# The FFN of a decoder block: four groups begin with one token half, weight blocks summed by DMA, outputs written by parts

## The chip, the cores and the metric

One Trainium2 chip, one of its cores. The metric is the device time of one execution in microseconds (us). Lower is better. Engine names as in the profile: PE is TensorE, DVE VectorE, ACT ScalarE, POOL GpSimd, SP SyncE. PE's clock has two levels, 2.4 and 1.2 GHz; the profile gives the granted share of the upper one.

## The reference, cut to what matters

The block is attention (two branches, gated, with a residual) followed by a SwiGLU FFN. B=1, 512 tokens, width 2048, FFN width 5632, all float32. Only the last part is touched:

```python
merged = sigmoid(gl_a) * (y_a @ w_proj_mla) + sigmoid(gl_b) * (y_b @ w_proj_sb)
x = x + gt1 * (merged @ w_out)
h2 = _rms(x, g_norm2) * (1 + sc2) + sh2
gate, up = jnp.split(h2 @ w_ffn_in, 2, axis=-1)
x = x + gt2 * ((silu(gate) * up) @ w_ffn_out)
```

## The kernel before

Both products of the FFN are done by one level of Strassen's scheme in Winograd's form: with the input split in blocks X11, X12 (first 256 tokens, lower and upper half of the channels), X21, X22 (second 256 tokens) and the weights in W11, W12, W21, W22, seven products of sums of blocks take the place of eight. The seven are named P1, P5, P7, P3, P6, P2, P4 in the order in which they run. P1 is X11 W11 and P2 is X12 W21, so P1 + P2 is one finished block, C11: the gate of the first token half. The other five need sums of blocks of both token halves (X[1] to X[4]) and four sums of weight blocks.

`ffn_in_group(g)` runs over 11 groups g of FFN columns (stage "a"); `ffn_out_chunk(ci, q)` over five chunks of groups, CH=((0,1,2),(3,4),(5,6),(7,8),(9,10)), times two halves q of the output columns (stage "b"). A **piece** is one 128x1024 weight tile of a product: 4 per product and group in stage a, one per product and group in stage b; 308 and 154 in all. For each piece SP loads a raw tile (512 KB, 10 buffers `rp2`), ACT casts it (`whi`), DVE computes the rest (`wlo` = raw - whi), and PE does 12 matmuls of 512 columns (`mm3`: three per product of a float32 pair of high and low parts). `ahead_to(i, 2, 6)` sets the order: tiles are made two pieces ahead and loaded six ahead; whi and wlo have three buffers each. For P5, P7, P6 and P4 `piece_make` first subtracts one raw tile from another on DVE, so each weight block is loaded once for its group and stays until its last use.

Between the pieces stand functions put in by `add_do`: bank copies, the gate times up, and `act_back1`/`act_back2`, which transpose a group's result, make its block sums and park them in DRAM (`apark`, stores by POOL); stage b fetches them (`yb`, by SP). `at_product(n, fn)` puts a function ahead of product n. With it the norms are placed: `norm2(k, th)` scales and shifts channel tile k of token half th, `x_sums(k)` makes X[1] to X[4] from two such tiles. `first_norms` does tiles 0 to 7 of the first half; `second_norms`, at product 3 (a piece counts as a product there), does everything else at once: 24 norms and 8 sets of sums. The transposes and final sums `out_tiles(q, col_)` come after all seven products of the last chunk for a q.

Names in rows: `x12h`, `x34h` and `x12l`, `x34l` are high and low parts of X[1], X[2] and of X[3], X[4]; `x` is the part of X11 and X12; `xr` the residual; `diag` belongs to the second half's rstd; `ps_s`, `ps_t`, `ps_mm`, `ps_y` are PSUM banks; `xo` the residual at the end. L82 is the helper that records every operation.

Of the kernel before, what the change touches and what calls it, by code (L numbers as in the profile page):

```python
# [87 lines left out]
def kernel(  # L88
# [982 lines left out]
    X = {}  # L1071

# [64 lines left out]
    raws = {}  # L1137
# [15 lines left out]
    def raw_load(key):  # L1153
        if key in raws:
            return
        r = st["rp2"].tile([P, 1024], F32, tag="raw2", name=nm("raw2"))
# [42 lines left out]
    cur = {"load": 0, "make": 0}  # L1199
# [43 lines left out]
    def ffn_in_group(g, order):  # L1243
        G = {}
        n = KD // 4

# [64 lines left out]
        product("P2", "A", False, True)  # L1311
# [62 lines left out]
    ffn_in_group(0, None)  # L1374
# [5 lines left out]

    at_product(1, lambda: last_sum(1))
    at_product(2, lambda: last_row(1))

    def second_norms():
        for k in range(8):
            norm2(k + 8, 0)
            norm2(k, 1)
            norm2(k + 8, 1)
            x_sums(k)
    at_product(3, second_norms)  # L1390
    for g in range(1, FG):
        ffn_in_group(g, None)
# [20 lines left out]
    def ffn_out_chunk(ci, q):  # L1413
# [17 lines left out]
        for prod in ORDER:  # L1431
# [21 lines left out]
    def finish(q, prod, t):  # L1453
        get = lambda n: acc[q, n, t]
        if prod == "P6":
            u = get("P6")
# [4 lines left out]
            c12 = get("P3")
            vec.tensor_tensor(c12, c12, u, ALU.add)
            fin[q, 2, 2, t], fin[q, 1, 2, t] = z, c12
        if prod == "P2":
            fin[q, 1, 1, t] = get("P2")
        if prod == "P4":
            c = get("P4")
            vec.tensor_tensor(c, c, get("P6"), ALU.add)
            fin[q, 2, 1, t] = c

    def out_tiles(q, col_):
        xr_ = {}
# [120 lines left out]
```

## Time and profile before

| | |
|---|---|
| median of 3 runs | 2693.76 us (2691.06 to 2694.64) |
| the profiled execution's own time | 2691.3 us |
| its span, first to last instruction | 2689.6 us |
| busy: PE, DVE, ACT, POOL | 96%, 75%, 43%, 6% of the span |
| FFN: stage a, stage b | about 1304 to 2230, 2230 to 2690 us |
| granted PE clock, mean | 0.985 |

Busy shares are means over the span. What a change in one stage is worth is read from that stage: which engine PE waits for there, and for how long.

### The profile page before, as it was taken

The page shows a single profiled execution, that of the slowest core. Times are in us where ns is not written, and L with a number is a line of the kernel's source. Part 1 is how long each engine was busy: PE and PEld are TensorE (multiplying, and loading weights), DVE is VectorE, ACT ScalarE, POOL GpSimd, SP SyncE. Part 2 cuts the span into 40 slices and gives each one's busy share as a digit, 9 for nine tenths or more (in the row PEclk, how much of TensorE's full clock was granted, in tenths as well). Part 3 has the DMA queues.
Part 4 walks back from the last instruction along what each step waited for, and adds up shares of the span by engine and source line. Part 5 has one row for each costly group of instructions (what it writes and reads, how often), then busy time and mean ns, then how long its engine had stood idle before and what let it go on. Part 6 is the DMA issues. An engine that isn't in the chain of part 4 may idle for free.

```text
span 2689.6 us, 32101 instructions
## 1 busy us (share of the span) xinstructions
PE 2584.3 (96%) x12166; PEld 2147.2 (80%) x12166; DVE 2024.8 (75%) x2614; ACT 1149.4 (43%) x1557; POOL 154.9 (6%) x256
## 2 busy tenths in 40 slices
PE   6999999999999999999779999999999999999997
PEld 4788888888899888888558888888888887888885
DVE  8966766657877854533768888888888887689997
ACT  4434655542333322222545544455544445543331
POOL 0000000000110100000001100111110111000001
PEclk9999999999999999999879999999999999999998
DMA  9854444336666783332325445445444549765562
GB/s 341 300 195 164 160 150 143 128 134 235 252 248 251 263 347 141 141 141 98 94 63 167 144 136 160 158 144 172 151 136 151 164 135 327 235 210 193 189 206 79
DMA packets 236579, 487.29 MB, mean 181 GB/s; under 512 B 15428, under 2 KB 159044, under 8 KB 211336
## 3 DMA queue, kind: packets, MB, share of 16 engines
q1 hardware_dynamic: 215552, 426.03, 46.5%
q0 software_dynamic: 14816, 48.51, 5.0%
q10 hardware_dynamic: 6056, 10.70, 1.0%
q8 instruction: 95, 1.56, 0.2%
q14 instruction: 60, 0.49, 0.1%
HBM read 425.93 MB, written 59.24 MB: 180 GB/s over the span
## 4 chain that ended last, share of the span: by engine, by line
PE 71%; issue 17%; DVE 6%; DMA 3%; ACT 2%; POOL 0%; SPq 0%; POOLq 0%; ACTq 0%; DVEq 0%
PE ps_mm L82 48%; PE ps_s L82 11%; PE ps_t L82 8%; PE ps_y L82 5%; DMA raw<-in_w_ff_dram 2%; DVE wlo L82 2%; DVE raw L271 1%; ACT whi L82 1%; DVE s L82 0%; DVE raw L82 0%; DMA gpark<-sg 0%; DMA raw<-in_w_ada_dram 0%; POOL out_dram L1487 0%; DVE x L82 0%; DVE xr L82 0%
## 5 line engine op out<-in xcount | busy, mean ns | idle before, releaser
L82 ACT CAST whi<-raw 128x1024 fp32r<-128x1024 f32 x672 | 702.8, 1050 | 1037.7 <-PE ps_mm L82 471.6
L82 DVE TENSOR_TENSOR wlo<-raw,whi 128x1024 fp32r<-128x1024 f32 x672 | 815.7, 1218 | 341.2 <-ACT whi L82 338.5
L82 DVE TENSOR_TENSOR raw<-raw,raw 128x1024 f32<-128x1024 f32 x264 | 319.2, 1220 | 20.9 <-DMA raw<-in_w_ff_dram 17.7
L82 PE MATMUL ps_mm<-hl,whi 128*128 128x512 f32 x832 | 327.2, 393 | 0.0
L82 PE MATMUL ps_mm<-hh,whi 128*128 128x512 f32 x832 | 325.0, 391 | 0.0
L82 PE MATMUL ps_mm<-hh,wlo 128*128 128x512 f32 x832 | 324.9, 390 | 0.0
L271 DVE CUSTOM_DVE_ANT_0 raw<-raw,cb,cols 128x2048 f32<-128x2048 f32 x96 | 224.5, 2344 | 0.7 <-DMA raw<-in_w_ada_dram 0.7
L82 PE MATMUL ps_s<-whi,x 128*128 128x512 f32 x704 | 218.6, 392 | 0.1
L82 PEld LDWEIGHTS ps_mm<-hh,wlo 128*128 128x128 f32 x832 | 156.2, 188 | 32.7
L82 PEld LDWEIGHTS ps_mm<-hl,whi 128*128 128x128 f32 x832 | 156.6, 188 | 30.4
L82 PEld LDWEIGHTS ps_mm<-hh,whi 128*128 128x128 f32 x832 | 156.4, 188 | 30.5
L82 PEld LDWEIGHTS ps_s<-whi,x 128*128 128x128 f32 x704 | 133.3, 189 | 28.1 <-DVE x L82 0.6
L82 PE MATMUL ps_s<-wlo,x 128*128 128x512 f32 x352 | 139.3, 396 | 1.8 <-ACT x L82 1.8
L82 PE MATMUL ps_mm<-whi,yb 128*128 128x512 f32 x440 | 137.0, 393 | 0.0
L82 PE MATMUL ps_s<-whi,yb 128*128 128x512 f32 x352 | 108.5, 389 | 0.0
L82 PE MATMUL ps_t<-whi,yb 128*128 128x512 f32 x352 | 108.5, 389 | 0.0
L82 PE MATMUL ps_mm<-whi,x 128*128 128x512 f32 x352 | 108.4, 389 | 0.0
L82 PE MATMUL ps_t<-wlo,x12h 128*128 128x512 f32 x176 | 74.0, 421 | 30.5 <-ACT x12h L82 30.5
L82 PE MATMUL ps_mm<-mgl,whi 128*128 128x512 f32 (+1 forms) x272 | 102.7, 377 | 0.0
L82 PE MATMUL ps_mm<-mgh,whi 128*128 128x512 f32 (+1 forms) x272 | 102.4, 377 | 0.0
L82 PE MATMUL ps_mm<-mgh,wlo 128*128 128x512 f32 (+1 forms) x272 | 102.4, 377 | 0.0
L82 PEld LDWEIGHTS ps_mm<-whi,yb 128*128 128x128 f32 x440 | 83.5, 190 | 17.5
(363 smaller groups left out, 5147.6 us busy)
## 6 DMA issues: line engine op xcount, KB each, us to landing
raw<-in_w_ff_dram SPq DMA_DIRECT2D x264, 512.0 KB, 5.4
raw<-in_w_ada_dram SPq DMA_DIRECT2D x96, 1024.0 KB, 5.1
yb<-apark SPq DMA_DIRECT2D x154, 256.0 KB, 5.7
raw<-in_w_gate_dram SPq DMA_DIRECT2D x27, 1024.0 KB, 4.9
raw<-in_w_sb_dram SPq DMA_DIRECT2D x24, 1024.0 KB, 4.9
raw<-in_w_out_dram SPq DMA_DIRECT2D x16, 1024.0 KB, 4.8
raw<-in_w_gate_dram SPq DMA_DIRECT2D x24, 512.0 KB, 4.9
raw<-in_w_lat_dram SPq DMA_DIRECT2D x8, 1024.0 KB, 8.2
```

Of the source, the lines that this page charges most:

```text
L82: ins = f(*a, **kw)
L271: tc.keep_in_program_order(nc.vector.tensor_tensor_reduce(raw, raw, cb, 1.0, col(C_B + 16 * ADA[name] + j), ALU.mult, ALU.add, dst))
```

## The change

There are three edits. **Early products.** NPRE = 4: for groups 0 to 3 P1 and P2 are run ahead of everything else of the FFN (E1, E2; order E1 of group 0, E1 of 1, E2 of 0, E2 of 1, then groups 2 and 3 alike): 32 pieces, which read the first token half alone. Their results (`p1` = P1, `s1` = silu of P1 + P2) are kept for group 0 and parked in DRAM (`epark`) for groups 1 to 3: 12 stores of 256 KB by POOL, 12 loads by SP. The norms are spread: the upper channel tiles of the first half over products 3 to 6, `second_norms(k)` one k at every third product from 7 on. The groups 0 to 3 then run F5, P7, P3, P6, P4, 20 pieces each; F5 is P5 with a load of W11 of its own. **Weight sums by DMA.** The subtractions on DVE (264) are gone. A tile of W11 gets W12, then W22, then W21 added by DMAs that POOL issues with `accum_op=ALU.add`, each after the tile's casts and before the next product's (P5, P6, P4); P7's tile is a load of W12 plus an add of W22. That is 264 adds in place of the subtractions and 16 for F5, and 16 loads more. Signs of the sums of X and of the result change with it (`ngt2` = -gt2). **Outputs.** In the last chunk the final sums are cut: `out_load` fetches the residual after P5 and P6; column half 1 and token half 1 of column half 0 are written after P2, the rest after P4, in 256-column tiles. PE has as many instructions as before.

```diff
+NPRE = 4
...
+    ngt2 = cp.tile([P, KD], F32, name="ngt2")
+    def minus_gt2():
+        vec.tensor_scalar(ngt2, ada["gt2"], -1.0, None, ALU.mult)
+    step(minus_gt2)
...
         s12, s34 = t2("s12"), t2("s34")
-        vec.tensor_tensor(s12[:, lo], a[:, hi], b[:, hi], ALU.add)
-        vec.tensor_tensor(s12[:, hi], s12[:, lo], a[:, lo], ALU.subtract)
+        vec.tensor_tensor(s12[:, lo], b[:, hi], a[:, hi], ALU.subtract)
+        vec.scalar_tensor_tensor(s12[:, hi], s12[:, lo], -1.0, a[:, lo], ALU.mult, ALU.subtract)
...
+    def raw_tile(key, r=None):
         src, km = raw_src(key)
-        sync_dma(r.rearrange("p (a b) -> p a b", b=128 if km else 256), src)
-        raws[key] = r
+        new = r is None
+        if new:
+            r = st["rp2"].tile([P, 1024], F32, tag="raw2", name=nm("raw2"))
+        dst = r.rearrange("p (a b) -> p a b", b=128 if km else 256)
+        if new:
+            sync_dma(dst, src)
+        else:
+            nc.gpsimd.dma_start(dst, src, accum_op=ALU.add)
+        return r
...
     PROD = {
-        "P1": ((1, 1), "11", None), "P5": (1, "12", "11"), "P7": (3, "22", "12"), "P3": (4, "22", None),
-        "P6": (2, "22", "11"), "P2": ((1, 2), "21", None), "P4": ((2, 2), "21", "22"),
+        "P1": ((1, 1), "a", "11", True), "P5": (1, "a", "+12", True), "P7": (3, "b", "12+22", False),
+        "P3": (4, "b", "22", False), "P6": (2, "a", "+22", True), "P2": ((1, 2), "b", "21", False),
+        "P4": ((2, 2), "a", "+21", False),
+        "E1": ((1, 1), "a", "11", False), "E2": ((1, 2), "b", "21", False),
+        "F5": (1, "a", "11+12", True),
     }
-    INTO = {"P5": "11", "P7": "12", "P6": "22", "P4": "21"}
-    LAST = {"P7": ("12",), "P6": ("11",), "P4": ("21", "22")}
-    def piece_keys(stage, g, prod, j):
-        _, x, y = PROD[prod]
-        return [(stage, g, b, j) for b in (y, x) if b]
-    def piece_make(stage, g, prod, j):
-        _, x, y = PROD[prod]
-        key = (stage, g, x, j)
-        if y:
-            kd = (stage, g, INTO[prod], j)
-            vec.tensor_tensor(raws[kd], raws[key], raws[stage, g, y, j], ALU.subtract)
-            key = kd
-        r = raws[key]
+    raws = {}
...
+    def piece_load(i):
+        stage, g, prod, j = pieces[i]
+        _, tl, blk, keep = PROD[prod]
+        if blk[0] != "+":
+            raws[i] = raw_tile((stage, g, blk[:2], j))
+    def piece_add(i):
+        stage, g, prod, j = pieces[i]
+        raw_tile((stage, g, PROD[prod][2][-2:], j), raws[i])
...
+    def piece_make(i):
+        stage, g, prod, j = pieces[i]
+        _, tl, blk, keep = PROD[prod]
+        key = (stage, g, blk[-2:], j)
+        r = raws.pop(i)
         hi = wp.tile([P, 1024], F32R, tag="whi", name=nm("whi"), bufs=3)
         lo = wp.tile([P, 1024], F32R, tag="wlo", name=nm("wlo"), bufs=3)
         v4 = lambda t: t.rearrange("p (k m c) -> p k m c", k=2, m=4)
         act.copy(v4(hi), kmc(key, r))
         vec.tensor_tensor(v4(lo), kmc(key, r), v4(hi).bitcast(F32), ALU.subtract)
-        for b in LAST.get(prod, ()):
-            del raws[stage, g, b, j]
+        if keep:
+            n = next(n for n in range(i + 1, len(pieces))
+                     if pieces[n][:2] == (stage, g) and pieces[n][3] == j and PROD[pieces[n][2]][2][0] == "+")
+            raws[n] = r
+            piece_add(n)
...
     def ahead_to(i, n_make, n_load):
-        while cur["load"] < min(i + n_load + 1, len(pieces)) or cur["make"] < min(i + n_make + 1, len(pieces)):
-            if cur["load"] <= cur["make"] or cur["load"] < min(i + n_load + 1, len(pieces)):
-                for key in piece_keys(*pieces[cur["load"]]):
-                    raw_load(key)
+        end = len(pieces)
+        while cur["load"] < min(i + n_load + 1, end) or cur["make"] < min(i + n_make + 1, end):
+            if cur["load"] < min(i + n_load + 1, end):
+                piece_load(cur["load"])
                 cur["load"] += 1
             else:
-                made[cur["make"]] = piece_make(*pieces[cur["make"]])
+                while cur["add"] < min(cur["make"] + 4, cur["load"]):
+                    if "+" in PROD[pieces[cur["add"]][2]][2][1:]:
+                        piece_add(cur["add"])
+                    cur["add"] += 1
+                made[cur["make"]] = piece_make(cur["make"])
                 cur["make"] += 1
...
+    def ffn_in_early(g, i):
+        G = groups.setdefault(g, {})
+        prod = ("E1", "E2")[i]
+        for j in range(KD // 4):
+            def use(w, j=j):
+                if i == j == 0:
+                    G["A"] = tb(*(("s", "s"), ("t", "t"))[g % 2])
+                for kk in range(2):
+                    prod_mm(G["A"], X[PROD[prod][0], 2 * j + kk], w, kk, i == 0 and j == 0 and kk == 0,
+                            i == 1 and j == KD // 4 - 1 and kk == 1)
+            add_piece(("a", g, prod, j), use)
+        def out():
+            for t in range(2):
+                x = t2(("p1", "s1")[i])
+                act.activation(x, G["A"][t], (AF.Copy, AF.Silu)[i])
+                if g > 0:
+                    nc.gpsimd.dma_start(epark[g, i, t], x)
+                else:
+                    G[("p1", "s1")[i], t] = x
+        add_do(out)
...
-        product("P1", "A", True, False)
-        copy_to("p1", "A")
-        if g > 0:
+        if early and g > 0:
+            add_do(lambda: fetch_early("p1"))
+        elif not early:
+            product("P1", "A", True, False)
+            copy_to("p1", "A")
+        if g > 0 and not early:
             add_do(lambda: act_back2(g - 1))
-        product("P5", "B", True, False)
+        product("F5" if early else "P5", "B", True, False)
         copy_to("z", "B")
+        if g > 0 and early:
+            add_do(lambda: act_back2(g - 1))
...
+        if not early:
+            product("P2", "A", False, True)
+        elif g > 0:
+            add_do(lambda: fetch_early("s1"))
         both(after_p2)
...
+    for g in range(0, NPRE, 2):
+        for i in range(2):
+            ffn_in_early(g, i)
+            ffn_in_early(g + 1, i)
+    for g in range(FG):
+        ffn_in_group(g, g < NPRE)
...
+    def second_norms(k):
+        norm2(k, 1)
+        norm2(k + 8, 1)
+        x_sums(k)
...
-    def second_norms():
-        for k in range(8):
-            norm2(k + 8, 0)
-            norm2(k, 1)
-            norm2(k + 8, 1)
-            x_sums(k)
-    at_product(3, second_norms)
-    for g in range(1, FG):
-        ffn_in_group(g, None)
+    for k in range(8):
+        at_product(3 + k // 2, lambda k=k: norm2(k + 8, 0))
+        at_product(7 + 3 * k, lambda k=k: second_norms(k))
...
+            if final and prod == "P5":
+                add_do(lambda: out_load(q, 1))
+            if final and prod == "P6":
+                add_do(lambda: out_load(q, 0))
+            if final and prod == "P2":
+                add_do(lambda: out_tiles(q, 1, (0, 1)))
+                add_do(lambda: out_tiles(q, 0, (0,)))
+            if final and prod == "P4":
+                add_do(lambda: out_tiles(q, 0, (1,)))
...
+            xr = xres[m]
+            cs = slice(256 * rows[0], 256 * rows[-1] + 256)
+            vec.scalar_tensor_tensor(xr[:, cs], o[:, cs], (ngt2 if col_ == 0 else ada["gt2"])[:, m:m + 1], xr[:, cs], ALU.mult, ALU.add)
+            (nc.gpsimd if q == 0 or rows[-1] == 0 else nc.sync).dma_start(outT[m * P:(m + 1) * P, cs], xr[:, cs])
...
-                for col_ in (1, 0):
-                    add_do(lambda q=q, col_=col_: out_tiles(q, col_))
```

**DVE, the norms and the sums of X.** Before, a stretch of the norms in group 0, at the sums of the second k (`xr` scaled and shifted, `s` and `x12l`, `x34l` the sums):

```order
L82 TENSOR_TENSOR x34l_10888<-s_1890_10878,x34h_10887 128x512
L82 SCALAR_TENSOR_TENSOR xr_9996<-xr_9996,ada_gs_182,rstd_10596 128x256
L82 SCALAR_TENSOR_TENSOR x_10892<-xr_10194,ada_sh_183,x_10892 128x256
L82 SCALAR_TENSOR_TENSOR x_10899<-xr_10194,ada_sh_183,x_10899 128x256
L82 SCALAR_TENSOR_TENSOR xr_10524<-xr_10524,ada_gs_182,rstd_10596 128x256
L82 SCALAR_TENSOR_TENSOR xr_10062<-xr_10062,ada_gs_182,rstd_10596 128x256
L82 TENSOR_TENSOR s_1897_10903<-xr_9666,xr_10194 128x256
L82 SCALAR_TENSOR_TENSOR xr_10592<-xr_10592,ada_gs_182,rstd_10596 128x256
L82 TENSOR_TENSOR s_1897_10903<-s_1897_10903,xr_9666 128x256
L82 TENSOR_TENSOR wlo_11077<-raw_1845_10628,whi_11076 128x1024
L82 TENSOR_TENSOR x12l_10908<-s_1897_10903,x12h_10907 128x512
L82 TENSOR_TENSOR s_1898_10904<-xr_9666 128x256
```

After, the sums of the first k:

```order
L83 TENSOR_TENSOR wlo_10981<-raw_1884_10860,whi_10980 128x1024
L83 SCALAR_TENSOR_TENSOR x_10999<-xr_10141,ada_sh_183,x_10999 128x256
L83 TENSOR_TENSOR wlo_11020<-raw_1889_10888,whi_11019 128x1024
L83 TENSOR_TENSOR s_1912_11003<-xr_10141,xr_9614 128x256
L83 SCALAR_TENSOR_TENSOR s_1912_11003<-s_1912_11003,xr_9614 128x256
L83 TENSOR_TENSOR wlo_11044<-raw_1896_10920,whi_11043 128x1024
L83 TENSOR_TENSOR x12l_11008<-s_1912_11003,x12h_11007 128x512
L83 TENSOR_TENSOR s_1913_11004<-xr_9614 128x256
L83 SCALAR_TENSOR_TENSOR s_1913_11004<-xr_10141,s_1912_11003 128x256
L83 TENSOR_TENSOR wlo_11062<-raw_1903_10950,whi_11061 128x1024
L83 TENSOR_TENSOR x34l_11014<-s_1913_11004,x34h_11013 128x512
```

Before, 39 rows stand between the `wlo` shown and the one ahead of it; after, a `wlo` stands behind every one to three rows of the norms.

**POOL, end of group 4 and start of group 5.** Before (`apark` stores of two column tiles, nothing else):

```order
L1328 DMA apark_322<-y34h_13562 128x2x256
L1328 DMA apark_322<-y34l_13563 128x2x256
L1328 DMA apark_323<-y1h_14029 128x2x256
L1328 DMA apark_323<-y1l_14030 128x2x256
L1328 DMA apark_324<-y1h_14042 128x2x256
L1328 DMA apark_324<-y1l_14043 128x2x256
L1358 DMA apark_323<-x_2510_14135 128x512
L1328 DMA apark_323<-y12h_14143 128x2x256
```

After (`raw` are the weight tiles that get an add):

```order
L1170 DMA raw_2550_14265<-in_w_ff_dram 128x4x256
L1170 DMA raw_2555_14287<-in_w_ff_dram 128x4x256
L1170 DMA raw_2492_13984<-in_w_ff_dram 128x4x256
L1170 DMA raw_2495_14002<-in_w_ff_dram 128x4x256
L1170 DMA raw_2500_14026<-in_w_ff_dram 128x4x256
L1394 DMA apark_336<-y1h_14109 128x2x256
L1394 DMA apark_336<-y1l_14110 128x2x256
L1394 DMA apark_337<-y1h_14122 128x2x256
L1170 DMA raw_2503_14044<-in_w_ff_dram 128x4x256
L1394 DMA apark_337<-y1l_14123 128x2x256
```

The first rows are the adds of P7 of group 5, the next three and the last but one those of its P5; the stores of `act_back1` of the group before, which wait for DVE, stand among them.

**DVE, the end of the program.** Before (`acc` sums of products, `xo` the residual, read from PSUM and scaled by gt2):

```order
L82 TENSOR_TENSOR acc_18758<-acc_18758,ps_mm_20992 128x512
L82 TENSOR_TENSOR acc_18760<-acc_18760,ps_mm_20993 128x512
L82 TENSOR_TENSOR acc_18758<-acc_18758,acc_18623 128x512
L82 TENSOR_TENSOR acc_18760<-acc_18760,acc_18625 128x512
L82 SCALAR_TENSOR_TENSOR xo_21170<-ps_mm_21178,ada_gt_184,xo_21170 128x512
L82 SCALAR_TENSOR_TENSOR xo_21172<-ps_y_21185,ada_gt_184,xo_21172 128x512
L82 SCALAR_TENSOR_TENSOR xo_21174<-ps_mm_21192,ada_gt_184,xo_21174 128x512
L82 SCALAR_TENSOR_TENSOR xo_21176<-ps_y_21199,ada_gt_184,xo_21176 128x512
L82 SCALAR_TENSOR_TENSOR xo_21206<-ps_mm_21214,ada_gt_184,xo_21206 128x512
L82 SCALAR_TENSOR_TENSOR xo_21208<-ps_y_21221,ada_gt_184,xo_21208 128x512
L82 SCALAR_TENSOR_TENSOR xo_21210<-ps_mm_21228,ada_gt_184,xo_21210 128x512
L82 SCALAR_TENSOR_TENSOR xo_21212<-ps_y_21235,ada_gt_184,xo_21212 128x512
```

After:

```order
L83 SCALAR_TENSOR_TENSOR xo_21086<-ps_mm_21268,ada_gt_184,xo_21086 128x512
L83 SCALAR_TENSOR_TENSOR xo_21088<-ps_y_21275,ada_gt_184,xo_21088 128x512
L83 SCALAR_TENSOR_TENSOR xo_21212<-ps_mm_21282,ngt_315,xo_21212 128x256
L83 SCALAR_TENSOR_TENSOR xo_21214<-ps_y_21287,ngt_315,xo_21214 128x256
L83 SCALAR_TENSOR_TENSOR xo_21216<-ps_mm_21292,ngt_315,xo_21216 128x256
L83 SCALAR_TENSOR_TENSOR xo_21218<-ps_y_21297,ngt_315,xo_21218 128x256
L83 TENSOR_TENSOR acc_18839<-acc_18839,ps_mm_21096 128x512
L83 TENSOR_TENSOR acc_18841<-acc_18841,ps_mm_21097 128x512
L83 SCALAR_TENSOR_TENSOR xo_21212<-ps_mm_21328,ngt_315,xo_21212 128x256
L83 SCALAR_TENSOR_TENSOR xo_21214<-ps_y_21333,ngt_315,xo_21214 128x256
L83 SCALAR_TENSOR_TENSOR xo_21216<-ps_mm_21338,ngt_315,xo_21216 128x256
L83 SCALAR_TENSOR_TENSOR xo_21218<-ps_y_21343,ngt_315,xo_21218 128x256
```

Before, eight tiles of 512 columns follow the last sums of products; after, four halves of 256 columns do, and the other tiles stand ahead of P4's two `acc` rows.

## Rows read from the trace of the kernel before

**Rows 1.** The page: busy time by engine; TensorE's busy tenths in 40 slices.
```profile
PE 2584.3 (96%) x12166; PEld 2147.2 (80%) x12166; DVE 2024.8 (75%) x2614; ACT 1149.4 (43%) x1557; POOL 154.9 (6%) x256
...
PE   6999999999999999999779999999999999999997
```

**Rows 2.** TensorE's waits, 1150 to 2690: total us, times, longest us.
```profile
PE ps_t L82 <- ACT x12h L82: 30.5, 7, 5.9
PE ps_mm L82 <- DVE wlo L82: 19.0, 15, 5.7
...
PE ps_y L82 <- DVE xo L82: 8.6, 5, 3.8
```

**Rows 3.** TensorE's timeline, start of the FFN: start, us, instruction, [wait before].
```profile
1304.25 0.28 PE L82 MATMUL ps_mm<-mgh,wlo 128*128 128x256 f32 x1
...
1306.31 0.50 PE L82 MATMUL ps_s<-wlo,x 128*128 128x512 f32 x1 [1.78 <-ACT x L82]
...
1317.82 1.19 PE L82 MATMUL ps_y<-diag,ones 128*128 128x256 f32 x2 [4.84 <-DVE diag L82]
...
1341.34 0.79 PE L82 MATMUL ps_t<-wlo,x12h 128*128 128x512 f32 x1 [5.85 <-ACT x12h L82]
...
1381.50 0.40 PE L82 MATMUL ps_mm<-wlo,x34h 128*128 128x512 f32 x1
```

**Rows 4.** Window: stretch, us, busy PE, PEld, DVE, ACT, POOL, clock, DMA, GB/s.
```profile
1301.40:1381.50 80.10, 42.58 (x129) 29.63 (x130) 66.91 (x134) 44.93 (x89) 0.54 (x1) 0.66 0.05 15
```

**Rows 5.** VectorE's lines by form, 1301.4 to 1381.5: busy, mean ns, idle before.
```profile
L82 DVE SCALAR_TENSOR_TENSOR xr<-xr,ada_gs,rstd 128x256 f32<-128x256 f32 x32 | 14.2, 477 | 0.1
L82 DVE TENSOR_TENSOR wlo<-raw,whi 128x1024 fp32r<-128x1024 f32 x10 | 12.2, 1216 | 4.0 <-ACT whi L82 4.0
L82 DVE TENSOR_TENSOR raw<-raw,raw 128x1024 f32<-128x1024 f32 x8 | 9.7, 1218 | 0.0
...
L82 DVE TENSOR_TENSOR x12l<-s,x12h 128x512 fp32r<-128x512 f32 x8 | 5.5, 689 | 3.8 <-ACT x12h L82 3.8
```

**Rows 6.** Windows of the FFN's two products (columns as in rows 4).
```profile
1400.00:2190.00 790.00, 778.32 (x3496) 640.97 (x3495) 664.01 (x736) 394.35 (x480) 96.74 (x140) 1.00 0.48 152
...
2300.00:2600.00 300.00, 300.00 (x1325) 248.43 (x1324) 259.96 (x264) 124.06 (x125) 0.00 (x0) 1.00 0.62 203
```

**Rows 7.** The page, groups of instructions: the subtractions of weight blocks.
```profile
L82 DVE TENSOR_TENSOR raw<-raw,raw 128x1024 f32<-128x1024 f32 x264 | 319.2, 1220 | 20.9 <-DMA raw<-in_w_ff_dram 17.7
```

**Rows 8.** DMA, 1400 to 2190: packets, MB, share of 16 engines; issue to landing.
```profile
q1 hardware_dynamic: 83300, 82.72, 34.5%
...
raw<-in_w_ff_dram SPq DMA_DIRECT2D x157, 512.0 KB, 5.9
...
apark<-y1h POOLq DMA_DIRECT2D x20, 256.0 KB, 2.6
```

**Rows 9.** DMA, 2300 to 2600: issue to landing.
```profile
raw<-in_w_ff_dram SPq DMA_DIRECT2D x64, 512.0 KB, 4.8
```

**Rows 10.** Windows with the fullest DMA engines (columns as in rows 4).
```profile
10.00:30.00 20.00, 6.13 (x14) 3.02 (x12) 18.54 (x40) 12.05 (x23) 0.68 (x1) 1.00 1.02 393
...
2230.00:2240.00 10.00, 10.00 (x53) 8.40 (x52) 10.00 (x13) 7.28 (x11) 2.85 (x4) 1.00 1.06 389
```

**Rows 11.** GpSimd's lines, 1295 to 2690: busy, mean ns of one issue.
```profile
L1328 POOL DMA_DIRECT2D apark<-y12l x22 | 15.8, 720 | 23.3 <-DVE y12l L82 23.3
```

**Rows 12.** Timelines of TensorE, SyncE and VectorE at the end.
```profile
2622.29 0.60 PE L82 MATMUL ps_mm<-consts,acc 128*128 128x128 f32 x4
...
2629.22 1.11 PE L82 MATMUL ps_y<-consts,acc 128*128 128x128 f32 x4
...
2669.54 0.63 PE L82 MATMUL ps_mm<-whi,yb 128*128 128x512 f32 x2
...
2675.33 2.25 SPq L178 DMA_DIRECT2D xo<-xpark  x4
...
2681.93 0.75 DVE L82 SCALAR_TENSOR_TENSOR xo<-ps_y,ada_gt,xo 128x512 f32<-128x512 f32 x1 [0.54 <-PE ps_y L82]
```

More of the change, by code (lines that the diff above doesn't have):

```diff
@@ L1090, in sums @@
         s12, s34 = t2("s12"), t2("s34")
-        vec.tensor_tensor(s12[:, lo], a[:, hi], b[:, hi], ALU.add)
-        vec.tensor_tensor(s12[:, hi], s12[:, lo], a[:, lo], ALU.subtract)
+        vec.tensor_tensor(s12[:, lo], b[:, hi], a[:, hi], ALU.subtract)
+        vec.scalar_tensor_tensor(s12[:, hi], s12[:, lo], -1.0, a[:, lo], ALU.mult, ALU.subtract)
         put(1, split_t(s12, "x12"))
         vec.tensor_tensor(s34[:, lo], a[:, lo], a[:, hi], ALU.subtract)
-        vec.tensor_tensor(s34[:, hi], b[:, lo], s12[:, hi], ALU.subtract)
+        vec.scalar_tensor_tensor(s34[:, hi], b[:, lo], -1.0, s12[:, hi], ALU.mult, ALU.subtract)
         put(3, split_t(s34, "x34"))
@@ L1151, in raw_src @@
         return src.rearrange("m p x -> p m x"), False
[L1153 to L1156, printed above, removed]
+    def raw_tile(key, r=None):
         src, km = raw_src(key)
-        sync_dma(r.rearrange("p (a b) -> p a b", b=128 if km else 256), src)
-        raws[key] = r
+        new = r is None
[7 more added lines that the diff above has]
+        return r
     def kmc(key, ap):
@@ L1198 @@
     made = {}
-    cur = {"load": 0, "make": 0}
+    cur = {"load": 0, "add": 0, "make": 0}
     pieces = []
@@ L1240, in tb, with ffn_in_group, fetch_early @@
         return [ps(t) for t in tags]
-    def ffn_in_group(g, order):
-        G = {}
+    def ffn_in_early(g, i):
[18 more added lines that the diff above has]
+        add_do(out)
+    def ffn_in_group(g, early):
+        G = groups.setdefault(g, {})
         n = KD // 4
+        def fetch_early(name):
+            for t in range(2):
+                G[name, t] = t2(name)
+                sync_dma(G[name, t], epark[g, ("p1", "s1").index(name), t])
         def product(prod, bank, start, stop):
@@ L1280, in after_p2 @@
         def after_p2(t):
-            s = t2("silu")
-            act.activation(s, G["A"][t], AF.Silu)
+            if early:
+                s = G.pop(("s1", t))
+            else:
+                s = t2("silu")
+                act.activation(s, G["A"][t], AF.Silu)
             vec.tensor_tensor(s, s, G["c12", t], ALU.mult)
@@ L1310, in ffn_in_group @@
         both(after_p6)
-        product("P2", "A", False, True)
+        if not early:
+            product("P2", "A", False, True)
+        elif g > 0:
+            add_do(lambda: fetch_early("s1"))
         both(after_p2)
@@ L1315, in ffn_in_group @@
         add_do(lambda: act_back1(g))
-        groups[g] = G
     groups = {}
+    epark = {(g, i, t): dp.tile([P, T], F32, name=f"epark_{g}_{i}_{t}")
+             for g in range(1, NPRE) for i in range(2) for t in range(2)}
     apark = [dp.tile([P, 7 * T], F32, name=f"apark_{i}") for i in range(2 * FG)]
@@ L1361, in act_back2 @@
             s12, s34 = t2("s12"), t2("s34")
-            vec.tensor_tensor(s12[:, lo], y2[:, lo], y2[:, hi], ALU.add)
-            vec.tensor_tensor(s12[:, hi], s12[:, lo], y1[:, lo], ALU.subtract)
+            vec.tensor_tensor(s12[:, lo], y2[:, hi], y2[:, lo], ALU.subtract)
+            vec.scalar_tensor_tensor(s12[:, hi], s12[:, lo], -1.0, y1[:, lo], ALU.mult, ALU.subtract)
             park(2 * g + j, 3, split_t(s12, "y12"))
             vec.tensor_tensor(s34[:, lo], y1[:, lo], y2[:, lo], ALU.subtract)
-            vec.tensor_tensor(s34[:, hi], y1[:, hi], s12[:, hi], ALU.subtract)
+            vec.scalar_tensor_tensor(s34[:, hi], y1[:, hi], -1.0, s12[:, hi], ALU.mult, ALU.subtract)
             park(2 * g + j, 5, split_t(s34, "y34"))
@@ L1463, in finish @@
             fin[q, 2, 2, t], fin[q, 1, 2, t] = z, c12
+            c = get("P4")
+            vec.tensor_tensor(c, c, u, ALU.add)
         if prod == "P2":
@@ L1466, in finish, with out_load, out_tiles @@
         if prod == "P4":
[L1467 to L1472, printed above, removed]
+            fin[q, 2, 1, t] = get("P4")
+    xres = {}
+    def out_load(q, col_):
         for i in range(4):
             m = 4 * (2 * q + col_) + i
-            xr = t2("xo")
-            sync_dma(xr, xpark[m])
-            xr_[i] = xr
+            xres[m] = t2("xo")
+            sync_dma(xres[m], xpark[m])
+    def out_tiles(q, col_, rows):
         for i in range(4):
@@ L1480, in out_tiles @@
             o = ps(("mm", "y")[i % 2])
-            for r in range(2):
+            for r in rows:
                 for t in range(2):
@@ L1484, in out_tiles @@
                                  fin[q, r + 1, col_ + 1, t][:, i * P:(i + 1) * P], ident)
-            xr = xr_[i]
-            vec.scalar_tensor_tensor(xr, o, ada["gt2"][:, m:m + 1], xr, ALU.mult, ALU.add)
-            (nc.gpsimd if m < 14 else nc.sync).dma_start(outT[m * P:(m + 1) * P, :], xr)
+            xr = xres[m]
+            cs = slice(256 * rows[0], 256 * rows[-1] + 256)
+            vec.scalar_tensor_tensor(xr[:, cs], o[:, cs], (ngt2 if col_ == 0 else ada["gt2"])[:, m:m + 1], xr[:, cs], ALU.mult, ALU.add)
+            (nc.gpsimd if q == 0 or rows[-1] == 0 else nc.sync).dma_start(outT[m * P:(m + 1) * P, cs], xr[:, cs])
     for ci in range(len(CH)):
```

3 lines of the change are left out of this document (removed).

## The prediction

> **What bounds the kernel now.** I read the page first: PE is busy for 96% of the span, and its row of tenths is full except at the start, at the end, and at one place in the middle, where two slices show 7 [rows 1]. So the question is only where PE stands still. The list of PE's waits from 1150 us on answers it: 30.5 us for `x12h` from ACT, 19.0 us for `wlo` from DVE, 8.6 us for `xo` at the end [rows 2]. The timeline of PE puts the first at the start of the FFN: the last matmul ahead of it starts at 1304.25, P1 of group 0 at 1306.3, then come waits for `diag` (4.84) and for one `x12h` after another, and the first matmul of P7 comes at 1381.50 [rows 3]. In that stretch DVE is busy for 66.9 of 80.1 us, the DMA engines for 0.05, and the granted clock is 0.66, between the two levels: PE waits, the clock falls to 1.2 GHz for a while, and the few matmuls that run take longer [rows 4]. Later, in the middle of stage a, PE is busy for 778 of 790 us and DVE for 664; in stage b PE for 300 of 300 and the DMA engines for 0.62 [rows 6]. A matmul takes 300/1325 = 0.2264 us, a piece of 12 of them 2.72 us; stage a is 308 pieces (838 us), stage b 154 (419 us). These 1257 us are untouched by the change, so what can be won is what PE waits.
>
> **The start of the FFN.** Before, 8 pieces (P1 and P5 of group 0) and 6 other matmuls take 1304.4 to 1381.5 = 77.1 us and need 8 x 2.72 + 6 x 0.2264 = 23.1: 54.0 us are lost. After, 32 pieces that need the first token half alone stand there, and the norms lie between them. PE has 32 x 2.72 = 87.1 us of work. DVE has the same norms, sums and copies as before, 66.9 - 12.2 (ten `wlo`) - 9.7 (eight subtractions) = 45.0 us [rows 4, 5], and 32 `wlo` at 1.22 = 39.0; 84.0 together. So the two are nearly even, and in my count PE sets the end. What stays of the loss: the first wait of 1.8, the wait for `diag` of 4.8, which comes from the evacuation of the second half and has no new cover, and some 3.4 for the half clock behind these and for slips: 10. Gain 54 - 10 = **44 us**. The margin is thin: DVE's own waits for ACT were 3.8 in the `x12l` rows and 4.0 in the `wlo` rows [rows 5]; in case all waits of this kind (with others, 13 us) return in full, and the clock falls for them, some 25 of the 54 are won.
>
> **The subtractions.** The 264 cost DVE 319.2 us, 1.22 each [rows 7]. In stage a DVE stands at 0.84 of the time [rows 6] and in b at 0.87, so most of them lie beside PE's work and their removal is worth only PE's waits for `wlo`, 19.0 us in all. The start of stage b (5.7 of them at once) and the tail keep part; I take **10**, at least 0, at most 17.
>
> **What the adds cost the DMA engines.** The trace of before has no accumulating DMA. The nearest row is the plain load of the same tile: 82.72 MB take 34.5% of the 16 engines over 790 us [rows 8], 3.30 us per MB, so 512 KB take p = 1.73 us of all 16. That is my lower bound. An add also has to read its target, so the upper bound is two such transfers, 3.46. Demand by stage, with PE's time beside it:
>
> - Groups 4 to 10: 0.48 x 76.2 = 36.6 us of loads and stores as now [rows 6] and 16 adds, for 28 pieces, 76.2 us. With the lower p 64.3, with the upper 92.
> - Groups 0 to 3: P1 and P2 are gone from the group (minus 4 loads net with F5's own, 6.9), `epark` adds 3.5: 33.2 and 16 adds, for 20 pieces, 54.4 us. 60.9 or 88.6.
> - Stage b, two groups at one q: 0.62 x 38.1 = 23.6 and 8 adds, for 38.1 us; 37.4 or 51.3; eleven such units.
>
> The fullest windows of the trace show a DMA share of 1.02 and 1.06 [rows 10], which I take as the ceiling: 80.8, 57.7 and 40.4 us. With the lower p only the early groups are over it, by 3.2 us each: 13 us. With the upper p 11.2, 30.9 and 10.9 us each are over: 7 x 11.2 + 4 x 30.9 + 11 x 10.9 = 322. Stage b tips at p = (40.4 - 23.6)/8 = 2.1 us, stage a at 2.8. I take the lower bound, as the row that it is nearest to is the load of the same bytes from the same tensor in the same shape: **13 us lost**.
>
> The Trainium skill bears on this. Its page "Collectives: The Full Stack", section "The bandwidth ceiling: the fold count and why AG ≠ RS ≠ AR", says that an add inside a DMA engine draws both operands through one read ring and so yields results at about half a copy's rate (62.28 against 32.35 GB/s). By it p would be near the upper bound and the change would lose. No run here shows it yet; the trace of before has plain transfers alone.
>
> **When the adds land.** An add starts when the casts of the tile's last use are done and must land before the next product's cast. In stage a a product has four pieces, so 10.5 us are left after the issue; in two-group chunks of stage b P5's tile is next used two pieces later, and I count 5.1 us from POOL's issue to the time when PE would wait. Loads land after 5.9 us in a and 4.8 us in b [rows 8, 9], stores by POOL after 2.6 [rows 8]. With 6 us for an add, as for the loads of stage a, each of the eight units that have two groups loses about 1 us: **8 us lost**, and 39 if an add lands after 10 us (8 x 4.9). POOL issues a 256 KB store in 0.72 us [rows 11]; at 0.72 to 1.44 us 16 adds take 12 to 23 us of a group's 76, so the queue itself has room. But it runs in order: an add behind an `apark` store waits until DVE has made what is stored, and the order shows the last add of P5 behind three such stores. P7's adds stand ahead of P5's; their tiles are loaded earlier, so I count nothing for it.
>
> **The end.** Before, the last product's last matmuls start at 2669.5, four `xo` loads are still issued at 2675.3, and the last tile's sum comes at 2681.9 [rows 12]; the program ends about 20 us after the last product. For q = 0 eight tiles took 8.0 us (2622.3 to 2630.3). After, four tiles of 512 columns and four of 256 lie ahead of P4, six tiles' worth at 1.0 us each; the last sum of them (0.6) runs beside P4's matmuls, so P4 starts 5.4 us later. Behind P4 stand four half tiles: an estimate of 1.6 for the two sums of the product, 0.4 to the first tile, 1.9 for four sums at the 0.48 of 256 columns [rows 5], and 6.9 from the last sum to the end as before; 10.8. 5.4 + 10.8 against 19.8 is 3.6 less, and the same split costs q = 0, whose tail lay beside other work, 0.9: **2.7, I take 2.5 us gained** (6 gained if the tiles ahead of P4 hide, 3 lost if DVE is late there). Signs, `minus_gt2` (16 columns, beside the matmuls of attention) and the parking of `epark` (12 stores, 0.72 us of POOL each) cost nothing that PE waits for; without this cover they would cost some 9 us.
>
> **The sum.** Against the profiled execution's 2691.3: -44 - 10 + 13 + 8 - 2.5 = -35.5, 2655.8. The median of the runs is 2.5 above that execution, so **2658** against 2693.8 (its own range 2640 to 2675).
>
> **The rivals.**
> - *The adds are wholly hidden*: no loss for early groups and landing: 2637. For it: the ceiling is passed by 6% only. Against: the early groups stand there with no margin.
> - *The start frees only 25 us*, as DVE and ACT pass their waits to each other: 2677. For it: 84.0 against 87.1.
> - *Adds land late* (10 us, in order behind stores): stage b stalls for 39 us in place of 8: 2689.
> - *An add costs the engines two transfers*: PE then waits for DMA in most groups. The loss grows by 152 us per us of p once stage b has tipped, and from p = 2.2 us on it is over 49 us (13 + 36) and the kernel slower than before. Half way, at 2.6 us, the early groups lose 17 each and the units of stage b 4, 112 in all: 2757. At 3.46: 2658 - 13 + 322 = 2967. The Trainium skill's page named above states this one. For it: an add needs its target's old content. Against: the plain load is a DRAM read, the target lies on chip.
> - *The edit doesn't do what it says* has no chance of its own: the counts of instructions follow from the order.
>
> **How the numbers follow.** My forecast 0.40; hidden 0.12; start at 25 us 0.08; late adds 0.13 (0.08 of it still faster, 0.05 within 0.2%); two transfers 0.27. 0.2% (5 us) is about what a measurement of this kernel can tell from no change. Faster 0.68, same 0.05, slower 0.27. The range from 2634, below the hidden case, to 2800 leaves out about half of the last rival.
>
> **What would show it.** Right: PE full from 1306 on but for two gaps; no subtractions on DVE and DVE near 0.6 in stage a; the DMA share near 0.85 in stage a and at 1.0 in groups 0 to 3; PE's waits of a few us for `whi` or `wlo` behind adds. Wrong: a share near 1.0 in the groups 4 to 10 with PE's granted clock below 1, adds that land after 10 us or more, or `wlo` waiting for ACT in the first 90 us of the FFN.

## The result and the profile after

The changed kernel takes **2930.65 us** (2929.9 to 2931.93) against 2693.25 for the kernel before: ratio 1.0883, interval 1.0864 to 1.0902, 237 us slower. The forecast was 2658.

The page after. PE's and the DMA engines' tenths in 40 slices of 73 us, then the groups of the casts' second half (`wlo`) and of the adds, then the transfers of weight tiles by queue (median us from issue to landing):

```profile
PE   6999999999999999999876798889999988887878
...
DMA  9845444266667734447999999999999999999994
...
L83 DVE TENSOR_TENSOR wlo<-raw,whi 128x1024 fp32r<-128x1024 f32 x672 | 816.4, 1220 | 841.4 <-ACT whi L83 834.5
...
L1170 POOL DMA_DIRECT2D raw<-in_w_ff_dram x264 | 339.0, 1402 | 891.3 <-DVE wlo L83 639.3
...
raw<-in_w_ff_dram SPq DMA_DIRECT2D x280, 512.0 KB, 8.7
raw<-in_w_ff_dram POOLq DMA_DIRECT2D x264, 512.0 KB, 11.4
```

The page counts 264 adds: F5's 16 stand in place of P5's in groups 0 to 3 and do not come on top, so there are 264 in all and not 280. The gap in PE's row at the start of the FFN is gone (slices 18 and 19), but from slice 20 on (1391 us) PE is below 9 in most slices, where the kernel before had a full row [rows 1], and the DMA engines are at 9 in every slice up to the last. Windows of the changed kernel (columns as in rows 4): the start of the FFN, the early groups, the late groups, stage b:

```profile
1300.00:1400.00 100.00, 93.30 (x416) 76.94 (x415) 84.36 (x151) 73.13 (x124) 12.06 (x14) 0.97 0.69 184
1400.00:1600.00 200.00, 146.48 (x588) 116.37 (x587) 82.96 (x99) 63.03 (x77) 68.93 (x64) 0.85 1.09 216
1600.00:2300.00 700.00, 620.36 (x2646) 503.70 (x2646) 378.65 (x452) 294.87 (x363) 244.21 (x240) 0.94 1.02 230
...
2450.00:2900.00 450.00, 376.84 (x1526) 300.35 (x1527) 229.42 (x257) 138.14 (x141) 89.89 (x81) 0.92 1.00 235
```

From 1400 us on DVE is at 0.4 to 0.55 of the time, where it was at 0.84 and 0.87 [rows 6], so it is not the bound; the DMA share is 1.0 or more in these windows, at a rate of only 216 to 235 GB/s, where the fullest windows before moved 389 and 393 [rows 10]. So the engines are full, yet they move little. PE's waits from 1150 us on:

```profile
PE ps_mm L83 <- DVE wlo L83: 116.1, 26, 12.4
PE ps_t L83 <- DVE wlo L83: 89.6, 35, 8.6
PE ps_mm L83 <- DVE xo L83: 12.8, 3, 8.8
PE ps_t L83 <- ACT s L83: 6.5, 1, 6.5
```

The seven waits for `x12h` (30.5 us) are gone, though one of 6.5 us, put down to `s`, stands ahead of the first matmul with `x12h`; those for `wlo` are 206 us in place of 19 [rows 2]. DVE is only the messenger: its `wlo` waits for ACT's `whi` (the page's 834.5 us). ACT waits in part for PE to free its buffers (158 us in four rows, none over 6.1 at once), which is the usual turn of the work; its largest single row, with the longest waits, is for the tile itself. That row, 1700 to 2200, then the queues (packets, MB, share of 16 engines) and landings there:

```profile
ACT whi L83 <- DMA raw<-in_w_ff_dram: 75.3, 26, 9.4
```

```profile
q0 software_dynamic: 53824, 67.09, 70.5%
q1 hardware_dynamic: 46805, 46.72, 30.8%
...
raw<-in_w_ff_dram POOLq DMA_DIRECT2D x93, 512.0 KB, 10.5
raw<-in_w_ff_dram SPq DMA_DIRECT2D x88, 512.0 KB, 7.7
```

Here is the price that the trace of before could not show. The software queue was busy for 0.705 x 500 = 352 us with 93 adds (48.8 MB) and 18.3 MB of stores. In the kernel before the same queue had stores alone, 1400 to 2190:

```profile
q0 software_dynamic: 11200, 36.71, 12.9%
```

That is 2.78 us per MB, so the stores are 51 us and an add (352 - 51)/93 = **3.24 us of all 16 engines**, where the load took 1.73.

### The profile page after: what moved, and what is told of

Same layout as the page of the kernel before. It is cut to its first block, busy times and chain, and to the rows that moved or that the text cites. A ratio compares the mean times of both kernels' runs of the same rounds, so it can differ in the third digit from the quotient of the medians.

```text
span 2929.3 us, 32695 instructions
## 1 busy us (share of the span) xinstructions
PE 2656.2 (91%) x12166; PEld 2187.4 (75%) x12166; DVE 1732.3 (59%) x2359; ACT 1140.0 (39%) x1557; POOL 503.0 (17%) x534
## 4 chain that ended last, share of the span: by engine, by line
DMA 17%; PE 14%; issue 12%; POOL 4%; DVE 3%; ACT 2%; SPq 0%; POOLq 0%; ACTq 0%; DVEq 0%
DMA raw<-in_w_ff_dram 15%; PE ps_t L83 5%; PE ps_mm L83 5%; POOL raw L1170 3%; PE ps_s L83 2%; DVE wlo L83 2%; DMA apark<-x 2%; ACT whi L83 2%; PE ps_y L83 1%; POOL apark L1394 1%; DMA yb<-apark 1%; DVE acc L83 1%; DMA xo<-xpark 0%; DVE s L83 0%; DVE xo L83 0%
## 5 line engine op out<-in xcount | busy, mean ns | idle before, releaser
L83 DVE TENSOR_TENSOR wlo<-raw,whi 128x1024 fp32r<-128x1024 f32 x672 | 816.4, 1220 | 841.4 <-ACT whi L83 834.5
L1170 POOL DMA_DIRECT2D raw<-in_w_ff_dram x264 | 339.0, 1402 | 891.3 <-DVE wlo L83 639.3
L83 PE MATMUL ps_s<-whi,x 128*128 128x512 f32 x576 | 178.8, 392 | 0.0
L868 POOL TENSOR_SCALAR_AFFINE_SELECT sa<-sa 128x128 f32<-128x128 f32 x32 | 17.3, 541 | 870.2 <-ACT sa L83 870.2
L83 PE MATMUL ps_mm<-whi,yb 128*128 128x512 f32 x440 | 148.5, 421 | 0.0
L83 PE MATMUL ps_mm<-wlo,yb 128*128 128x512 f32 x220 | 94.9, 431 | 42.0 <-DVE wlo L83 40.4
L83 PEld LDWEIGHTS ps_s<-whi,x 128*128 128x128 f32 x576 | 109.2, 190 | 22.8 <-DVE x L83 0.2
L83 PE MATMUL ps_mm<-wlo,x34h 128*128 128x512 f32 x176 | 76.1, 433 | 49.3 <-DVE wlo L83 49.3
L83 PE MATMUL ps_s<-wlo,x 128*128 128x512 f32 x288 | 114.2, 396 | 1.8 <-ACT x L83 1.8
L83 PE MATMUL ps_t<-wlo,yb 128*128 128x512 f32 x176 | 74.7, 425 | 38.8 <-DVE wlo L83 38.6
L83 PEld LDWEIGHTS ps_mm<-whi,yb 128*128 128x128 f32 x440 | 91.3, 208 | 20.1
## 6 DMA issues: line engine op xcount, KB each, us to landing
raw<-in_w_ff_dram POOLq DMA_DIRECT2D x264, 512.0 KB, 11.4
```

The costliest lines, as they stand in the source:

```text
L83: ins = f(*a, **kw)
L868: nc.gpsimd.affine_select(a[:, dg], a[:, dg], pattern=[[-1, P]], compare_op=ALU.is_gt, fill=0.0, base=0, channel_multiplier=1)
L1170: nc.gpsimd.dma_start(dst, src, accum_op=ALU.add)
```

## The experiments

**Theory A**: an add costs the engines nearly two transfers, and they are the bound. **Theory B**: the adds come late by their order in POOL's queue and by what they wait for. Ratios are to the kernel before on the same chip. The runs were made on four chips (e1, e3, e4; e2, e5, e6; e7a, e7_best, e8; e9, e10), where the kernel before took 2691.6 to 2693.5 us, so 2 us between runs of different chips mean nothing.

**e1_plain**, the same issues without the addition:

```diff
-            nc.gpsimd.dma_start(dst, src, accum_op=ALU.add)
+            nc.gpsimd.dma_start(dst, src)
```

> The changed kernel with each of the 280 adds issued as a plain load of the same block into the same tile, from the same queue and after the same waits; it leaves out the weight sums (the products use the last block alone). Theory A, an add costs the 16 engines about two transfers (from the trace after, 1700 to 2200: 70.5% of 500 us for 93 adds and 18.1 MB of stores, so 3.25 us each) and the engines are the bound: at the load's 1.75 us the groups fit again, 2650 to 2680 us. Theory B, the adds are late by the order in POOL's queue and by their waits, whatever they cost the engines: the order and the waits are the same here, so it stays above 2850.

Measured **2662.76 us**, ratio 0.9887 (0.9859 to 0.9916). Order, queue, waits and bytes fetched are those of the changed kernel (264 loads in place of 264 adds); the addition is gone, and with it all of the loss. Two things go along with it: POOL's issue is shorter (a median of 0.75 us in place of 1.29, which leaves POOL far from busy in either), and the packets are larger, which e4 takes apart. Queues and landings of this kernel, 1700 to 2100, and its window:

```profile
q0 software_dynamic: 17409, 61.35, 47.4%
...
raw<-in_w_ff_dram POOLq DMA_DIRECT2D x81, 512.0 KB, 5.8
```

```profile
1700.00:2100.00 400.00, 400.00 (x1806) 331.82 (x1805) 255.22 (x299) 200.50 (x244) 109.35 (x151) 1.00 0.81 261
```

81 plain loads take (189.6 - 52.5)/81 = 1.69 us each, and PE is full. The first matmul of group 4 and of stage b tell where the changed kernel loses against this one. Timeline of PE, changed kernel first:

```profile
1734.43 0.48 PE L83 MATMUL ps_s<-wlo,x 128*128 128x512 f32 x1
...
2357.51 0.48 PE L83 MATMUL ps_s<-wlo,yb 128*128 128x512 f32 x1
```

```profile
1649.45 0.47 PE L83 MATMUL ps_s<-wlo,x 128*128 128x512 f32 x1
...
2197.51 0.47 PE L83 MATMUL ps_s<-wlo,yb 128*128 128x512 f32 x1
```

85 us are lost in the early groups, 75 in the late ones, 108 after (spans 2929.3 and 2660.9). The prediction's own sum with p = 3.24 gives 109, 53 and 100: 262 against 268, so the total fits better than its parts.

**e3_noearly**, `NPRE = 0`, the norms at product 3:

> The changed kernel with NPRE = 0: adds by DMA and outputs by parts, no early products, the norms all at product 3 as before. If the parts are independent, it is slower than the changed kernel by the 44 us that the early products were to win: 2975. Theory A: groups 0 to 3 have 28 pieces of PE work again in place of 20 to hide the same 16 adds, so 27.5 us a group become 7.8; 11 groups of 7.8 and eleven units of 9.2 in stage b are 187, with 54 lost at the start as before: 2870 to 2890.

Measured **2882.15 us** (two runs, 15 us apart), ratio 1.0702 (1.0635 to 1.077): as theory A has it. With the adds the early products cost about 48 us; by theory A because they take PE's work away from beside the adds.

**e4_fat**, the adds from rows of 4 KB:

```diff
-            nc.gpsimd.dma_start(dst, src, accum_op=ALU.add)
+            nc.gpsimd.dma_start(r, fat_src(key), accum_op=ALU.add)
```

> The changed kernel with the adds reading rows of 4 KB in place of 1 KB (same bytes, other weights, so the sums are those of wrong blocks). Theory A in the form that bytes decide: an add stays at 3.2 us and the time at 2930. If the packets decide (512 of 1 KB each per add): the price falls to half or less, and the time to 2650 to 2750.

Measured **2822.81 us** (two runs, 16 us apart), ratio 1.0482 (1.0409 to 1.0554): between the two. Queue, 1700 to 2100:

```profile
q0 software_dynamic: 16573, 58.32, 65.1%
...
raw<-in_w_ff_dram POOLq DMA_DIRECT2D x77, 512.0 KB, 9.5
```

An add costs (260.4 - 49.9)/77 = 2.73 us. With some 80 packets to a store (11200 for 140 in the kernel before), this queue has about 144 packets to an add here, as many to a plain load in e1, and about 520 to an add in the changed kernel. So of the 1.55 us between 1.69 and 3.24, the small packets hold 0.5 and the addition itself 1.0, if the plain load would cost the same from rows of 4 KB, which no run shows.

**e2_dve**: early products and split outputs, sums on DVE (`vec.tensor_tensor(..., ALU.add)` in `piece_make`, blocks loaded as before). **e5_p7** adds 50 adds to it:

```diff
+        if prod == "P5" and by_dma(stage, g, "P7"):
+            src, km = raw_src((stage, g, "22", j))
+            nc.gpsimd.dma_start(raws[stage, g, "12", j].rearrange("p (a b) -> p a b", b=256), src, accum_op=ALU.add)
```

**e6_dve_tail** is e2_dve with the old `out_tiles`.

> Early products and outputs by parts as in the change, but the weight sums on DVE as before (264 of them and 16 for F5, no adds by DMA). Theory A: the whole loss came with the adds, so 2693 - 44 - 2.5 = 2647, 2640 to 2665. If the early products themselves lose (DVE and ACT late at the start, or 8 more loads a group): 2670 or more.

> e2_dve with one kind of sum moved to DMA: that of P7, in groups 4 to 10 and in stage b (50 adds of 280), where the engines have room: 36.6 + 4 x 3.25 = 49.6 of 76 us in a group, 23.6 + 2 x 3.25 = 30.1 of 38 in a unit of stage b. Theory A: no loss, and up to 5 us less than e2_dve for DVE's relief. Theory B (adds land late whatever the load): over 10 us slower than e2_dve, with PE waiting for wlo at P7.

> e2_dve with the outputs as before, all eight tiles of a q after P4 and their loads late: 2 to 4 us slower than e2_dve if the split of the outputs wins what was counted, the same if it does not.

Measured **2663.0** (ratio 0.9888, 0.9874 to 0.9903), **2653.05** (0.985, 0.9835 to 0.9864) and **2658.75** (0.9872, 0.9855 to 0.9888). Without adds the change gains 30 us, so the early products are worth having; 50 adds where there is room gain 10 more; and the outputs edit loses 4 where it was to win. The price of an add is not one of crowded engines: in e5 the engines are at 0.65 from 1700 to 2100 and PE is full (its window stands below), and by the same count its 20 adds there cost (118.8 - 51.0)/20 = 3.39 us each:

```profile
q0 software_dynamic: 16160, 28.84, 29.7%
```

PE at the end of e2_dve:

```profile
2638.54 0.60 PE L83 MATMUL ps_y<-consts,acc 128*128 128x128 f32 x4
2643.88 1.12 PE L83 MATMUL ps_mm<-consts,acc 128*128 128x128 f32 x4 [4.74 <-DVE xo L83]
2644.79 1.06 PE L83 MATMUL ps_y<-consts,acc 128*128 128x128 f32 x4
```

and its windows:

```profile
2640.00:2650.00 10.00, 5.80 (x20) 4.21 (x21) 7.79 (x12) 1.05 (x1) 0.76 (x2) 0.60 0.30 118
2646.00:2650.00 4.00, 3.68 (x12) 2.47 (x13) 2.44 (x5) 0.00 (x0) 0.76 (x2) 0.50 0.43 167
```

The third tile waits 4.7 us for a bank that DVE has yet to read, because DVE is still at the `wlo` and sums ahead. After this wait the granted clock is 0.50, the lower level, into the last product (0.60 is the mean of the ten us); the same wait (4.72) stands at the end of q = 0.

**e8_p5p7** (P5's sums by DMA as well) and **e9_p5** (P5's alone):

```diff
+        if prod == "P1" and by_dma(stage, g, "P5"):
+            src, km = raw_src((stage, g, "12", j))
+            nc.gpsimd.dma_start(raws[stage, g, "11", j].rearrange("p (a b) -> p a b", b=256), src, accum_op=ALU.add)
```

> e5_p7 with the sums of P5 by DMA as well, in groups 4 to 10 and in stage b (100 adds of 280). Theory A: 36.6 + 8 x 3.25 = 62.6 of 76 us in a group, 23.6 + 4 x 3.25 = 36.6 of 38.1 in a unit of stage b: still under the ceiling, so within 5 us of e5_p7 (2648 to 2658). Theory B, or a two-piece lead that is too short in stage b: eight units of some 5 us, 2690.

> e2_dve with the sums of P5 alone by DMA in groups 4 to 10 and stage b (50 adds, as many as e5_p7 has for P7). If the adds of P5 are late by their place (issued at P1's casts, beside the stores of the group before, with two to four pieces to land): most of the 85 us that e8_p5p7 lost against e5_p7 come back, 2700 or more. If it took both kinds to overfill the engines: like e5_p7, 2650 to 2665.

Measured **2737.85** (1.0171, 1.0155 to 1.0186) and **2709.74** (1.0063, 1.0049 to 1.0076). Theory A alone misses this, and e8 is 48 us above theory B's 2690 too; e9 came out as its first branch had it, with adds that are late by their place. e9 has as many adds as e5 and takes 57 us more, with engines that have room in the mean. Windows, e9 first, then e5:

```profile
1700.00:2100.00 400.00, 385.63 (x1700) 316.91 (x1699) 304.96 (x344) 191.65 (x235) 74.82 (x90) 0.98 0.63 175
...
1728.00:1734.00 6.00, 6.00 (x33) 5.05 (x31) 4.24 (x5) 3.65 (x6) 4.15 (x5) 1.00 1.19 251
```

```profile
1700.00:2100.00 400.00, 400.00 (x1805) 331.90 (x1805) 324.36 (x363) 202.31 (x244) 75.22 (x90) 1.00 0.65 180
```

In e9 P5's adds are issued between 1718 and 1731, among the stores of the group before; ACT then waits for one of these tiles:

```profile
1739.83 1.05 ACT L83 CAST whi<-raw 128x1024 fp32r<-128x1024 f32 x1 [4.12 <-DMA raw<-in_w_ff_dram]
```

The engines are at 1.19 for six microseconds in which the tiles should land. PE has pieces in stock and does not stop here: its gap comes 15 us later, at a piece of P7. DVE's `wlo` are late behind ACT's wait, SP issues its next loads only behind one of them, and P7's sum then waits for such a load. SP, DVE, PE:

```profile
1744.58 2.58 SPq L179 DMA_DIRECT2D raw<-in_w_ff_dram  x2
...
1751.24 1.23 DVE L83 TENSOR_TENSOR raw<-raw,raw 128x1024 f32<-128x1024 f32 x1 [3.81 <-DMA raw<-in_w_ff_dram]
...
1754.93 0.77 PE L83 MATMUL ps_mm<-wlo,x34h 128*128 128x512 f32 x1 [4.30 <-DVE wlo L83]
```

So room in the mean of a group does not tell whether an add lands in time, and a late one can cost PE at another product. How much of the delay is the crowd and how much the order in the queue was not taken apart, and this chain was followed in one group only.

**e7a_tail_early_loads** (the old output tiles, the residual loaded early), **e7_best** (and P7's sums by DMA everywhere), **e10_p7_late** (P7's sums by DMA but not in the early groups):

> e6_dve_tail (early products, sums on DVE, all output tiles after P4) with one part of the outputs edit back: the residual is loaded after P5 and P6 of the last chunk. If the late loads cost what DVE waited for them in e6 (3.59 and 0.70 us at the end): 4 us less than e6, 2655. If the split of the tiles and not the loads was the edit's worth: no change.

> e7a with the sums of P7 by DMA in all groups and in stage b (66 adds). Theory A: the early groups carry 33.2 + 4 x 3.25 = 46.2 us in 54.4 of PE's time, so no loss; DVE, 0.95 busy there, gets 4.9 us a group back. e5_p7 (2653) less 4 for the tail, 4 for the loads and 4 to 8 for the early groups: 2637 to 2645. If adds land late there: 2650 or more.

> e7a_tail_early_loads with P7's sums by DMA only in groups 4 to 10 and in stage b. If the adds in the early groups are what e7_best paid for, 2644 to 2648; if those groups do not matter, as e7_best, 2652.

Measured **2654.46** (0.9861, 0.9847 to 0.9876), **2652.19** (0.985, 0.9833 to 0.9866) and **2644.3** (0.9817, 0.9804 to 0.9831). e7a is 4 us under e6, but on another chip, and their intervals overlap. With the early loads in both, e7a is 9 us under e2, so the cut of the output tiles itself costs more than the edit as a whole, some 7 us by the ratios. e7_best missed what was expected and takes 8 us more than e10_p7_late, from which it differs by the adds of groups 0 to 3 alone. The groups themselves are not slower for them. First matmul of group 0 behind the early products and first of group 4, e7_best, then e10_p7_late:

```profile
1411.91 0.50 PE L83 MATMUL ps_t<-wlo,x12h 128*128 128x512 f32 x1 [0.88 <-ACT s L83]
...
1649.38 0.47 PE L83 MATMUL ps_s<-wlo,x 128*128 128x512 f32 x1
```

```profile
1404.94 0.50 PE L83 MATMUL ps_t<-wlo,x12h 128*128 128x512 f32 x1 [0.88 <-ACT s L83]
...
1641.87 0.47 PE L83 MATMUL ps_s<-wlo,x 128*128 128x512 f32 x1
```

Both take 237 us for the four groups. The loss of 7 us stands ahead of them, at the end of the early products, where PE waits 4.31 and 1.74 us for `wlo` and the first adds are issued among the `epark` stores. POOL and PE in e7_best:

```profile
1391.34 1.48 POOL L1209 DMA_DIRECT2D raw<-in_w_ff_dram  x1 [9.39 <-DMA raw<-in_w_ff_dram]
1392.25 1.70 POOL L1278 DMA_DIRECT2D epark<-p  x2
...
1392.58 0.80 PE L83 MATMUL ps_s<-wlo,x 128*128 128x512 f32 x1 [4.31 <-DVE wlo L83]
```

e10_p7_late is 49 us faster than the kernel before.

## Why the prediction was wrong

**The step that failed** is "I take the lower bound": p = 1.73 us for an add, by the row of the plain load. It measured 3.24, close to the upper bound of 3.46, and the rival "an add costs the engines two transfers", held at 0.27, is what happened. Its mechanism held: at p = 3.24 the three demands give 109 + 53 + 100 = 262 in place of 13, so 2658 - 13 + 262 = 2907, 24 under the measured time; these 24 were not taken apart. At the price that it took, the forecast nearly comes out: e1, with 1.69 us a load, takes 2662.8 us against 2658, so the other terms were off by 5 us in sum, though not each. The row was nearest by bytes, tensor and shape, but not by kind: none of its transfers was an addition. Between ends this far apart, with the change on the wrong side of zero from p = 2.2 on, the range had no ground to stop at 2800. The rule of the Trainium skill's page "Collectives: The Full Stack", section "The bandwidth ceiling: the fold count and why AG ≠ RS ≠ AR", is measured on collectives between four ranks (a ReduceScatter, which adds, at 32.35 GB/s against 62.28 for an AllGather, which copies: a ratio of 1.93). The changed kernel is close to it, 3.24/1.73 = 1.87. Part of that is luck: with as many packets to an add as to a load (e4 against e1) the ratio is 2.73/1.69 = 1.62, and the rest went with the small packets. That the addition costs the engines is shown; why it costs them 1.0 us, the second read or something else, no run here shows.

**The start of the FFN** was right up to 1402 us. PE's timeline of the changed kernel:

```profile
1306.68 0.50 PE L83 MATMUL ps_s<-wlo,x 128*128 128x512 f32 x1 [1.78 <-ACT x L83]
...
1317.52 1.19 PE L83 MATMUL ps_y<-diag,ones 128*128 128x256 f32 x2 [4.52 <-DVE diag L83]
...
1391.26 0.39 PE L83 MATMUL ps_t<-wlo,x 128*128 128x512 f32 x1
```

The last four of the 32 pieces start at 1391.26 and take 10.9: 1402.1 - 1306.7 = 95.4 us for 87.1 of work, so with the first wait 10 of the 54 lost us stay, as counted, 4.52 of them for `diag`. Right behind it PE waits 6.5 us ahead of the first `x12h` matmul (1408.77), while DVE waits 6.9 for a store of `epark` among the first adds; e1 has no wait there. Nor was the start the whole price of the edit: with sums on DVE e6 gains 34.4 in all, not 44. In the 20-piece groups DVE has nearly all of its time taken (the window from 1400 to 1620 of e2_dve, then of the kernel before):

```profile
1400.00:1620.00 220.00, 210.41 (x935) 170.23 (x934) 200.46 (x229) 105.92 (x129) 30.19 (x44) 1.00 0.61 199
1400.00:1620.00 220.00, 217.21 (x980) 179.29 (x979) 183.53 (x204) 110.50 (x135) 26.90 (x39) 1.00 0.46 145
```

PE lacks 9.6 of 220 us there, 2.8 before. The stall at the norms had gone in part to the groups that were made shorter.

**The subtractions**: 10 forecast, 10 measured (e2 to e5, on one chip), but that is luck in part: the forecast was for all 264, and these are the 50 of P7 in the late groups and stage b. There PE's waits for `wlo` stood at P7: 8.7 us in e2 from 1645 to 2180, none in e5. With all 264 moved at a plain load's price (e1) the time is that of e2, so nothing is gained in all.

**When the adds land**: 6 us was assumed; the median is 11.4 in the changed kernel, 6.5 in e5 with free engines. The rival "adds land late" is not needed for the changed kernel, since the same order with cheap transfers (e1) shows none of its loss; it is a loss of its own in e8 and e9, and may be in e7_best.

**The end**: 2.5 us gain forecast, 4 us loss measured (e2 against e6). The count had the tiles ahead of P4 at their own pace; it left out that DVE reaches them behind the `wlo` of P4, and the clock that PE's wait costs.

## What to carry to other kernels

Price an operation by a row of its kind, and where the trace has none, measure it alone first: one run with the addition left out would have decided this case. Moving work from an engine that is not the bound to the DMA engines paid here only in stretches where these have room, so move it sum by sum (50 adds gained 10 us, 264 lost 268 against plain loads) and look at the DMA share of the very microseconds in which each must land, and at what stands beside it in its queue. Work that is pulled forward to fill a gap is taken from where it covered something else; look at what is left there.

## What was not expected of the hardware

The plain load by the software queue went in about 144 packets (3.6 KB each in the mean), the add from the same 1 KB rows in about 520. An add from 4 KB rows took 2.73 us of the engines in place of 3.24, and still 1.6 times the 1.69 of a plain load in as many packets. POOL issued an add in 1.29 us and the plain load of the same bytes in 0.75 (medians).
